# Three contraction steps of the down stage's first product placed beside the last channel tile, in place of one

## The chip, the cores and the metric

The kernel runs on one core of a Trainium2 chip. The metric is the device time of one execution in microseconds (us): the median of the runs of a kernel. Beside the timed runs there is one profiled execution, whose trace gives the rows quoted below; the times in them count from the start of its span.

## The reference

One encoder layer over two request groups (256 and 1024 tokens, model width 1024). The part that matters here is its last piece, a gated feed-forward block with a width-3 convolution along the tokens between its two products:

```
def conv_ffn(h, w_up, w_conv, b_conv, w_down):
    up = h @ w_up                                  # (tokens, 2 * 2816)
    up = lax.conv_general_dilated(up, w_conv...)   # depthwise, width 3, + b_conv
    gate, val = jnp.split(up, 2, axis=-1)
    return (jax.nn.silu(gate) * val) @ w_down      # (tokens, 1024)
...
h = rmsnorm(x, g_pre_ffn[l]) * (1 + scale2) + shift2
y = conv_ffn(h, w_up[l], w_conv[l], b_conv[l], w_down[l])
x = x + gate2 * rmsnorm(y, g_post_ffn[l])
```

All data are float32.

## The kernel before

Each float32 matmul operand is split into a high and a low part (`split`, lines 89 to 91: ScalarE, ACT, rounds the high part; VectorE, DVE, or GpSimd, POOL, subtracts it from the source for the low part), and TensorE (PE) makes three products of the parts. So one operand costs one instruction on ACT and then one on DVE or POOL.

**The up stage** goes over 22 channel tiles f of 128 channels, in the order 10 to 21 and then 0 to 9. For each tile four 256 KB pieces of `w_up` are loaded into four rotating slots (`raw`, 4 in all), sums of them are formed (`S`), and both are split into weight operands `ws`, which rotate through 8 slots (6 in the pool `wr`, 2 in `sf`). PE then makes seven products of 12 matmuls (line 1210), a Strassen-like scheme over two 512-token halves, in the order X(11), Y(12), X(S2), V(S1), X(S3), V(S4), X(22). X and V are accumulated on, and each intermediate state is read out by ACT or DVE (lines 1217 to 1233) before PE adds the next product to it: lines 1217 and 1223 copy X to `ug`, 1225 copies V to `uv`, 1227 adds X to `uv`, 1229 adds V to `ug`. While PE is at the next tile, ACT and DVE do convolution, SiLU and gating (`ag`, `av`, lines 1043 to 1245), and the result `av` is stored to `g_d[f]` in DRAM (line 1076). The last tile is f = 9; its store goes by POOL's queue.

**The down stage** makes seven more Strassen-like products (M3, M5, M1, M7, M4, M2, M6; line 1153), each of 11 contraction steps k and 5 token tiles j, 3 matmuls for each pair, so 15 matmuls for a step. Step k of the first product, M3, takes A00_k (loaded from `g_d[2k]`, 320 KB) and the difference of two 256 KB blocks of `w_down`, `raw_d01_k` and `B11_k`. Its operands are `aoM3_k` and `boM3_k`. The `A00` and `B11` tiles stay in memory for the later products. They lie in the pool `dr`, which is opened over the space of the pools `wr`, `wp`, `er` and others that the up stage has done with; the pool `dn` (the tiles `xo`, `G2`, `y`) is opened over `sf`.

**The early step.** For k = 0 of M3 the A tile is loaded as `ea_0` as soon as tile 0 is stored, and the two blocks of `w_down` as `raw_e` behind the loads of the last channel tile. `early_split` makes the operands `eao_0` and `ebo_0` in `er`, and PE runs the 15 matmuls right behind the last product of f = 9, while ACT and DVE still work on the convolution of f = 9. After that PE goes on with step 1.

**What sets the order.** PE runs in the order of the source. In this part the order on ACT, DVE, POOL and in the DMA queue of SyncE (SP) is chosen by a scheduler when the kernel is built. Each queue is worked through in order, so that an instruction that waits holds up all that stand behind it. Tiles that are opened over other tiles wait for the last use of these.

## Time and profile before

| | |
|---|---|
| median of 3 runs | 1454.65 us (1453.76 to 1455.06) |
| the profiled execution: its time, its span | 1453.5 us, 1451.8 us |
| PE busy | 1377.5 us, 95% of the span |
| DVE, ACT, POOL busy | 1031.5, 677.9, 546.8 us |
| granted TensorE clock, mean of the span | 0.980 |

In the rows, `start us, us` are the start and the length of a group of equal instructions; `[1.92 <-ACT uv L1225]` says that the engine stood idle for 1.92 us before them, until the named instruction ended. `PEld` is the loading of weights into PE, `SPq`, `ACTq` and `POOLq` are DMAs issued by those queues; the length in a DMA's row is that of its issue, not of its transfer. A row of stretches gives for each engine its busy time and in brackets the number of instructions, then the granted clock, the busy share of the DMA engines and what they moved.

### The profile page before, as it was taken

To read this page: it belongs to the slowest core of one execution; us is meant where nothing else is said; L and a number is where in the kernel's file an instruction comes from. 1 tells how busy PE (TensorE), PEld (TensorE's weight loads), DVE (VectorE), ACT (ScalarE), POOL (GpSimd) and SP (SyncE) were. 2 spreads that over 40 slices of the span, in tenths; PEclk is the share of its full clock that TensorE was granted. 3 is DMA by queue.
4 is the path that set the end of the run, shared out by engine and by line. 5 is a ranking of instruction groups with operands and counts; after the bars stand their busy time and mean duration, and the time that the engine had idled before them with its cause. 6 is when DMAs were issued, how large, how long until landed. Compare 5 with 4: busy or idle time off the path is not lost. (4 is left out here: it accounts for less than half of the span.)

```text
span 1451.8 us, 20330 instructions
## 1 busy us (share of the span) xinstructions
PE 1377.5 (95%) x7057; PEld 1132.6 (78%) x7057; DVE 1031.5 (71%) x1619; ACT 677.9 (47%) x1379; POOL 546.8 (38%) x664
## 2 busy tenths in 40 slices
PE   8999989898999999888999999999999989999996
PEld 6786667676788788877888888887888768888875
DVE  5675667878845456896657566678788576996777
ACT  3543465644433333565444454544555345533632
POOL 3346755787764111434333333344444100000301
PEclk9999999999999999999999999999999999999998
DMA  9657542332233632552221212122222478365764
GB/s 287 218 211 268 184 151 74 111 111 69 83 105 113 215 112 83 168 150 83 80 63 61 82 59 84 56 92 67 84 87 87 147 245 299 106 197 178 161 206 163
DMA packets 178011, 195.91 MB, mean 135 GB/s; under 512 B 12152, under 2 KB 132020, under 8 KB 175604
## 3 DMA queue, kind: packets, MB, share of 16 engines
q1 hardware_dynamic: 170760, 176.83, 37.9%
q10 hardware_dynamic: 5468, 14.38, 2.9%
q0 software_dynamic: 1680, 3.41, 1.3%
q8 instruction: 55, 0.90, 0.3%
q14 instruction: 48, 0.39, 0.1%
HBM read 156.55 MB, written 38.03 MB: 134 GB/s over the span
## 5 line engine op out<-in xcount | busy, mean ns | idle before, releaser
L1153 PE MATMUL dn<-boM,aoM 128*128 128x512 f32 x1140 | 268.2, 398 | 8.9 <-ACT boM L90 5.1
L1153 PEld LDWEIGHTS dn<-boM,aoM 128*128 128x128 f32 x1140 | 218.5, 192 | 58.6 <-ACT boM L90 6.4
L91 POOL TENSOR_TENSOR ws<-raw_s,ws 128x512 fp32r<-128x512 f32 x56 | 88.5, 1584 | 166.0 <-ACT ws L90 165.0
L91 POOL TENSOR_TENSOR ws_S<-S,ws_S 128x512 fp32r<-128x512 f32 x66 | 102.0, 1547 | 128.2 <-ACT ws_S L90 128.1
L1210 PE MATMUL upX<-bop_T,ws_S 128*128 128x512 f32 x528 | 130.5, 397 | 6.2 <-ACT ws_S L90 3.3
L1210 PEld LDWEIGHTS upX<-bop_T,ws_S 128*128 128x128 f32 x528 | 100.0, 191 | 27.7 <-ACT ws_S L90 3.5
L338 PE MATMUL ps_ga<-w_a,h1hi 128*128 128x512 f32 x320 | 104.6, 404 | 5.4 <-POOL w_a L91 4.4
L338 PE MATMUL ps_gb<-w_b,h1hi 128*128 128x512 f32 x320 | 105.0, 409 | 1.6 <-DVE w_b L91 1.1
L90 ACT ACTIVATE ws_S<-S 128x512 fp32r<-128x512 f32 x88 | 54.8, 629 | 76.7 <-PE upX L1210 27.6
L1043 DVE SCALAR_TENSOR_TENSOR ag<-ug,c,ag 128x1023 f32<-128x1023 f32 x44 | 67.7, 1540 | 24.1 <-ACT ag L1047 23.3
L338 PEld LDWEIGHTS ps_ga<-w_a,h1hi 128*128 128x128 f32 x320 | 59.3, 191 | 25.1 <-issue 6.7
L1201 PEld LDWEIGHTS upQ<-hp,ws 128*128 128x128 f32 x576 | 72.3, 191 | 1.9
L90 ACT ACTIVATE ws<-raw_s 128x512 fp32r<-128x512 f32 x78 | 48.6, 626 | 52.6 <-issue 26.2
L1201 PE MATMUL upQ<-hp,ws 128*128 128x256 f32 x576 | 72.8, 283 | 0.0
L1097 PE MATMUL upP<-hp,wp 128*128 128x256 f32 x480 | 62.1, 290 | 11.2 <-DVE wp L91 8.3
L1097 PEld LDWEIGHTS upP<-hp,wp 128*128 128x128 f32 x480 | 59.7, 196 | 13.3 <-DVE wp L91 9.5
L1178 DVE TENSOR_TENSOR S<-raw_s,raw_s 128x512 f32<-128x512 f32 x44 | 53.7, 1221 | 22.1 <-DMA raw_s<-in_w_up_dram 18.2
L90 ACT ACTIVATE aoM<-saM 128x640 fp32r<-128x640 f32 x55 | 40.4, 738 | 62.1 <-issue 24.5
L338 PEld LDWEIGHTS ps_gb<-w_b,h1hi 128*128 128x128 f32 x320 | 57.8, 191 | 14.6 <-issue 2.6
L97 POOL TENSOR_TENSOR rstd<-ms,mhalf 128x2 f32<-128x2 f32 (+1 forms) x90 | 65.7, 730 | 7.3
L880 PE MATMUL y<-wo,mh 128*128 128x512 f32 x160 | 64.0, 400 | 2.1 <-ACT mh L794 2.1
L1210 PE MATMUL upV<-bop,ws_S 128*128 128x512 f32 x264 | 63.6, 390 | 1.9 <-ACT uv L1225 1.9
(289 smaller groups left out, 3227.8 us busy)
## 6 DMA issues: line engine op xcount, KB each, us to landing
raw_d<-in_w_down_dram SPq DMA_DIRECT2D x103, 256.0 KB
raw_s<-in_w_up_dram SPq DMA_DIRECT2D x88, 256.0 KB
A<-g_d SPq DMA_DIRECT2D x66, 320.0 KB
wa<-in_w_ada_dram SPq DMA_DIRECT2D x16, 1024.0 KB
g_d<-av SPq DMA_DIRECT2D x21, 512.0 KB
raw_p<-in_w_up_dram SPq DMA_DIRECT2D x40, 256.0 KB
wa<-in_w_ada_dram SPq DMA_DIRECT2D x16, 512.0 KB
vr_d<-vr SPq DMA_DIRECT2D x20, 256.0 KB
```

The lines of the kernel that those rows point to most:

```text
L90: nc.scalar.activation(w[:, 0, :], raw, AF.Copy)
L91: (eng or nc.gpsimd).tensor_tensor(out=w[:, 1, :], in0=raw, in1=w[:, 0, :].bitcast(F32), op=ALU.subtract)
L97: nc.gpsimd.tensor_tensor(out=r, in0=ms, in1=mhalf.to_broadcast([P, n]) if n > 1 else mhalf, op=ALU.pow)
L338: nc.tensor.matmul(ps, st, mv, start=(i == 0), stop=(i == n - 1))
L880: nc.tensor.matmul(ys[n], mh[:, kt, :], wos[(kt, n)][:, 0, :], start=(i == 0), stop=False)
L1043: nc.vector.scalar_tensor_tensor(out=acc[:, o:o + b - a], in0=src[:, a:b], scalar=c2[:, i, fi:fi + 1], in1=acc[:, o:o + b - a], op0=ALU.mu ...
L1097: nc.tensor.matmul(ps[:, half, :], st, hp[:, hi, kt, :], start=(kt == 0 and i == 0 and half == 0), stop=(kt == KT - 1 and i == 2), skip_gr ...
L1153: nc.tensor.matmul(ps, ao[ai][:, cs_], w[wi], start=(k == 0 and q == 0), stop=(k == NK - 1 and q == 2))
L1178: nc.vector.tensor_tensor(out=s, in0=a, in1=b, op=op)
L1201: nc.tensor.matmul(Q[:, half, :], st, hp[:, hi, kt, :], start=(kt == 0 and i == 0 and half == 0), stop=(kt == KT - 1 and i == 2), skip_gro ...
L1210: nc.tensor.matmul(ps, w[:, wi, P * j:P * j + P], bops[(b, j)][:, hi, :], start=(start and j == 0 and i == 0), stop=(stop and j == 3 and i ...
```

## The change

`NE`, the number of early steps, goes from 1 to 3. The two operand parts of the A tile lie in `er` for k = 0 and 1 and in two slots of the pool `wp` for k = 2 (weight slots that the up stage no longer uses). The operand of the weights, `ebo_k`, takes the next of the 8 rotating `ws` slots in place of a place of its own in `er`. `ea` stays a single buffer, so the three A tiles follow each other through it.

```
-    NE = 1
+    NE = 3
...
     def early_split():
         for k, (a, b) in enumerate(eops):
             nc.vector.tensor_tensor(out=b[0], in0=b[0], in1=b[1], op=ALU.subtract)
-            ao = er.tile([P, 2, 640], F32R, name=f"eao_{k}")
-            bo_ = er.tile([P, 2, 512], F32R, name=f"ebo_{k}")
-            split(ao, a, nc.vector)
+            if k < 2:
+                t = er.tile([P, 2, 640], F32R, name=f"eao_{k}")
+                ao = [t[:, h, :] for h in range(2)]
+            else:
+                ao = [wp.tile([P, 2, 512], F32R, tag="w", name=f"eao{'hl'[h]}_{k}", bufs=5)
+                      .rearrange("p a c -> p (a c)")[:, 0:640] for h in range(2)]
+            bo_ = ws_slot(f"ebo_{k}")
+            nc.scalar.activation(ao[0], a, AF.Copy)
+            nc.vector.tensor_tensor(out=ao[1], in0=a, in1=ao[0].bitcast(F32), op=ALU.subtract)
             split(bo_, b[0], nc.vector)
-            eops[k] = [[t[:, h, :] for h in range(2)] for t in (ao, bo_)]
+            eops[k] = [ao, [bo_[:, h, :] for h in range(2)]]
+
+    def ws_slot(name):
+        i = wstate["i"] % 8
+        wstate["i"] += 1
+        return fslot(name) if i < 6 else sf.tile([P, 2, 512], F32R, tag="w", name=name, bufs=2)
...
         def wop(name, src, eng=None):
-            if wstate["i"] % 8 < 6:
-                w = fslot(f"ws{f}_{name}")
-            else:
-                w = sf.tile([P, 2, 512], F32R, tag="w", name=f"ws{f}_{name}", bufs=2)
-            wstate["i"] += 1
+            w = ws_slot(f"ws{f}_{name}")
             split(w, src, eng)
             wops[name] = w
```

Seven lines are added ahead of the later code, so line 1217 before is 1224 in the change, and so on. The scheduler moves instructions at three places. The number in a name after the step or tile counts tiles and can be passed over; `[waits ...]` names the counters that the instruction waits for: an engine's, or one of the eight of the hardware DMA queues (`DMAHW`) and of the software ones (`DMASW`).

The first place is ACT in the up stage, where it works for tiles 3 and 4. Before:

```order
L90 ACTIVATE ws4_S4_10067<-S4_4_10065 128x512 [waits DVE_49,PE_49]
L90 ACTIVATE ws4_22_10070<-raw_s4_11_10041 128x512 [waits DMAHW4_49,PE_49,Pool_49]
L1047 ACTIVATE ag3_10025<-ug3_9932,c2_5061 128x1024 [waits DVE_49,Activation_49]
L1233 ACTIVATE uv3_9933<-upX_3_9929 128x512 [waits PE_49]
L90 ACTIVATE ws5_11_10188<-raw_s5_00_10179 128x512 [waits DMAHW5_49]
L1047 ACTIVATE av3_10026<-uv3_9933,c2_5061 128x1024 [waits DMAHW2_49,Activation_49]
L1243 ACTIVATE ag3_10025<-ag3_10025 128x1024 [waits DVE_49]
```

In the change:

```order
L90 ACTIVATE ws4_S4_10067<-S4_4_10065 128x512 [waits DVE_49,PE_49]
L1144 ACTIVATE eao_1_10918<-ea_1_10772 128x640 [waits DMAHW1_49]
L90 ACTIVATE ws4_22_10070<-raw_s4_11_10041 128x512 [waits DMAHW4_49,PE_49,Pool_49]
L1047 ACTIVATE ag3_10025<-ug3_9932,c2_5061 128x1024 [waits DVE_49,Activation_49]
L1240 ACTIVATE uv3_9933<-upX_3_9929 128x512 [waits PE_49]
L90 ACTIVATE ws5_11_10188<-raw_s5_00_10179 128x512 [waits DMAHW5_49]
L1047 ACTIVATE av3_10026<-uv3_9933,c2_5061 128x1024 [waits DMAHW2_49,Activation_49]
L1250 ACTIVATE ag3_10025<-ag3_10025 128x1024 [waits DVE_49]
L1224 ACTIVATE ug4_10076<-upX_4_10073 128x512 [waits PE_49]
```

The high part of `eao_1` now stands between `ws4_S4` and `ws4_22`; its low part stands on DVE at the same place, ahead of the addition that ends `ug3`. The load of `ea_1` is issued by SP two loads behind the store of tile 2, for whose landing it waits. `eao_0` stands in both kernels two tiles earlier, between `ws2_S4` and `ws2_22`.

The second place is DVE beside tiles 8 and 9, where `raw_e` is subtracted. Before:

```order
L1178 TENSOR_TENSOR S4_9_10794<-raw_s9_01_10757,S2_9_10781 128x512 [waits DMAHW2_49,Pool_49]
L1136 TENSOR_TENSOR raw_e0_0_10768<-raw_e0_0_10768,raw_e0_1_10769 128x512 [waits DMAHW6_49,DMAHW7_49,DVE_49,Pool_49]
L91 TENSOR_TENSOR ebo_0_10900<-raw_e0_0_10768,ebo_0_10900 128x512 [waits Activation_49]
L91 TENSOR_TENSOR ws9_S3_10791<-S3_9_10789,ws9_S3_10791 128x512 [waits PE_49,Activation_49]
L1227 TENSOR_TENSOR uv8_10653<-upX_8_10649,uv8_10653 128x512 [waits PE_49]
```

In the change:

```order
L1185 TENSOR_TENSOR S4_9_10806<-raw_s9_01_10757,S2_9_10793 128x512 [waits DMAHW4_49,Pool_49]
L1136 TENSOR_TENSOR raw_e0_0_10768<-raw_e0_0_10768,raw_e0_1_10769 128x512 [waits DMAHW0_49,DMAHW1_49,DVE_49,Pool_49]
L91 TENSOR_TENSOR ws9_S3_10803<-S3_9_10801,ws9_S3_10803 128x512 [waits PE_49,Activation_49]
L1136 TENSOR_TENSOR raw_e1_0_10774<-raw_e1_0_10774,raw_e1_1_10775 128x512 [waits DMAHW3_49,DMAHW4_49,DVE_49,Pool_49]
L1234 TENSOR_TENSOR uv8_10653<-upX_8_10649,uv8_10653 128x512 [waits PE_49]
```

The split of `ebo_0` is gone from here (it stands some rows lower, and on ACT behind the copies of V and X of tile 8, no longer ahead of that of V), and the subtraction of `raw_e1` has come in ahead of the addition that reads X of tile 8. One half of `raw_e1` takes the slot of `raw_e0_1`, so its load waits for the subtraction two rows higher.

The third place is the SP queue at the change of stages. Before:

```order
L1076 DMA g_d8_72<-av8_10746 128x2x512 [waits DVE_49]
L1293 DMA A00_1_10983<-g_d2_66 128x640 [waits DMAHW6_49,PE_49]
L1308 DMA B11_1_10984<-in_w_down_dram 128x512
L1293 DMA A00_2_10981<-g_d4_68 128x640 [waits DMAHW0_49]
L1308 DMA B11_2_10982<-in_w_down_dram 128x512 [waits DMAHW1_49]
```

In the change:

```order
L1076 DMA g_d8_72<-av8_10746 128x2x512 [waits DMAHW2_49,DVE_49]
L1315 DMA raw_d01_6_11134<-in_w_down_dram 128x512 [waits DMAHW3_49,DVE_49]
L1372 DMA xo1_13289<-out_0_dram 128x1024 [waits DMAHW2_49,DMAHW5_49,DMASW2_49,DVE_49]
L1300 DMA A00_3_11040<-g_d6_70 128x640 [waits PE_49]
L1315 DMA B11_3_11041<-in_w_down_dram 128x512 [waits DMAHW7_49]
L1300 DMA A00_4_11038<-g_d8_72 128x640 [waits DMAHW0_49,PE_49]
```

A 512 KB load for the end of the kernel, `xo1`, has come in ahead of the first A tile of M3. Its place in memory is that of `av9`, the last channel tile's result, and `DMASW2_49` counts the landing of the store of `g_d9` from it. `A00_1` waited for PE's first reading of `ws9_12`, early in tile 9. `A00_3` lies over the slot of `eaoh_2`, and what it waits for on PE is the last but one of the 45 early matmuls; `A00_4` waits for the last.

## The prediction

> **What bounds the kernel now.** I read the page's busy times and costliest groups first:

> ```profile
> PE 1377.5 (95%) x7057; PEld 1132.6 (78%) x7057; DVE 1031.5 (71%) x1619; ACT 677.9 (47%) x1379; POOL 546.8 (38%) x664
> L1153 PE MATMUL dn<-boM,aoM 128*128 128x512 f32 x1140 | 268.2, 398 | 8.9 <-ACT boM L90 5.1
> ```

> TensorE (PE) is the bound, so only its idle time and its slow clock can be won or lost. In the down products 5.1 of 8.9 us idle end with ACT's `boM`. The timeline of PE shows where:

> ```profile
> 1157.74 2.88 PE L1210 MATMUL upX<-bop_T,ws 128*128 128x512 f32 x12
> 1160.46 3.56 PE L1153 MATMUL dn<-ebo,eao 128*128 128x512 f32 x15
> 1168.56 46.77 PE L1153 MATMUL dn<-boM,aoM 128*128 128x512 f32 x191 [4.54 <-ACT boM L90]
> ```

> Call 1160.46 t0. A row's length runs to the modelled end of its last matmul; starts are the safe measure: 12 matmuls take 1160.46 - 1157.74 = 2.72, so 0.2267 each at full rate. After the early step PE waits 4.54 us for step 1. The view by stretches shows what follows (PE first; the granted clock is the third figure from the end):

> ```profile
> 1168.56:1175.00 6.44, 6.44 (x14) 4.76 (x15) 5.27 (x9) 2.40 (x4) 0.00 (x0) 0.50 0.94 318
> ```

> PE restarts at clock 0.50: 14 matmuls in 6.44 us where 3.17 would do, so 3.27 lost. The hand-over thus holds 4.54 + 3.27 = 7.8 us to be won. It is the place the change goes for; two more waits in the up stage must be read, since instructions for the early steps lie in those queues.

> **Hand-over to M3.** Before, 45 matmuls (k = 0 to 2) were through at 1175.00 + 16 x 0.2267 = 1178.63, t0 + 18.2. In the change k = 0 to 2 run without a pause, to t0 + 45 x 0.2267 = t0 + 10.2 plus the last one's tail, 10.4. Step 3 must then be ready. But `A00_3` lies over `eaoh_2`, and SP issues it only at the last but one early matmul, about t0 + 10.5; ahead of it in SP stands `xo1`, waiting for the store of `g_d9`:

> ```profile
> 1165.28 1.23 DVE L1245 TENSOR_TENSOR av<-ag,av 128x1024 f32<-128x1024 f32 x1
> 1166.81 0.81 POOL L1076 DMA_DIRECT2D g_d<-av  x1 [28.60 <-DVE av L1245]
> g_d<-av POOLq DMA_DIRECT2D x1, 512.0 KB, 3.6
> ```

> The store lands at 1166.81 + 3.6 = 1170.4 = t0 + 10.0: nearly the same time, so both waits would have to go. Behind the issue come the load and the operands. How long a 320 KB load takes is seen at `ea` of tile 0 (SP, then its readers on ACT and DVE; the store ahead of it too):

> ```profile
> 993.75 0.37 SPq L1076 DMA_DIRECT2D g_d<-av  x1
> 997.80 0.34 SPq L1128 DMA_DIRECT2D ea<-g_d  x1
> 1000.90 0.74 ACT L90 ACTIVATE eao<-ea 128x640 fp32r<-128x640 f32 x1 [3.48 <-DMA ea<-g_d]
> 1001.68 0.82 DVE L91 TENSOR_TENSOR eao<-ea,eao 128x640 fp32r<-128x640 f32 x1 [4.19 <-ACT eao L90]
> ```

> Load: 1000.90 - 997.80 = 3.1. Store of 512 KB to the load that waits for it: 4.05. From the A tile to PE, the rows of step 1:

> ```profile
> 1166.43 0.82 DVE L91 TENSOR_TENSOR aoM<-A,aoM 128x640 fp32r<-128x640 f32 x1
> 1167.16 0.68 DVE L1330 TENSOR_TENSOR sbM<-raw_d,B 128x512 f32<-128x512 f32 x1
> 1167.88 0.63 ACT L90 ACTIVATE boM<-sbM 128x512 fp32r<-128x512 f32 x1 [2.93 <-DVE sbM L1330]
> ```

> 0.74 on ACT, then 1168.56 - 1166.43 = 2.13: 2.9 in all. Lower bound of the start of k = 3: t0 + 10.5 + 3.1 + 2.9 = 16.5. With `xo1`'s 512 KB moved first, 4.05 - 3.1 = 0.95 more: 17.5. Upper: G2, 1 MB, which ACT now issues early, since `aoM` of steps 1 and 2 no longer stands ahead of it, shares the DMA engines: 19.3. Its own passage before is seen in ACT's queue, in SP and among the waits:

> ```profile
> 1167.89 0.36 ACTq L1267 DMA_DIRECT2D G<-gate_d  x1
> SPq L1293 <- DMA G<-gate_d: 5.8, 1, 5.8
> 1176.68 0.33 SPq L1293 DMA_DIRECT2D A<-g_d  x1
> ```

> So G2 takes 1176.68 - 1167.89 = 8.8 us beside other loads. I take t0 + 17.6, a pause of 7.2 in place of 4.54. Work done, that is 0.6 ahead of before; but the slow restart, which before lay inside these 45 matmuls, now comes behind them. It cost 3.27 there; at tile 2, below, 3.42 us at half clock lost 1.7. Middle 2.5. **Term: -0.6 + 2.5 = +1.9**, from 16.5 - 18.2 + 1.7 = 0 to 19.3 - 18.2 + 3.3 = +4.4.

> **Tile 4: the split of `eao_1`.** Before has the same thing once, for `eao_0`:

> ```profile
> 1004.75 2.88 PE L1210 MATMUL upY<-bop,ws 128*128 128x512 f32 x12
> 1009.62 4.22 PE L1210 MATMUL upX<-bop_T,ws_S 128*128 128x512 f32 x12 [1.99 <-ACT ug L1217]
> 1013.64 2.65 PE L1210 MATMUL upV<-bop_T,ws_S 128*128 128x512 f32 x9
> 1011.15:1014.57 3.42, 3.42 (x10) 2.68 (x9) 3.42 (x3) 0.69 (x2) 2.62 (x2) 0.50 0.00 0
> 1004.48 3.52 DVE L1043 SCALAR_TENSOR_TENSOR ag<-ug,c,ag 128x1023 f32<-128x1023 f32 x2 [0.78 <-ACT ag L1047]
> ```

> ACT waited 3.48 and DVE 4.19 for `ea_0`; everything behind (the taps of `ag`, SiLU, the copy `ug`) came late, and PE stood 1.99 before X(S2). Half clock followed. X(S2) should have started at 1007.47, V at 1010.19; V came at 1013.64: 3.45 lost, 2.15 stall and 1.3 clock. The change adds this for tile 2. There before was:

> ```profile
> 1035.76 0.37 SPq L1076 DMA_DIRECT2D g_d<-av  x1
> 1041.48 0.69 DVE L1229 TENSOR_TENSOR ug<-upV,ug 128x512 f32<-128x512 f32 x1 [2.03 <-PE upV L1210]
> 1043.82 2.60 DVE L1043 SCALAR_TENSOR_TENSOR ag<-ug,c,ag 128x1023 f32<-128x1023 f32 x2 [0.93 <-ACT ag L1047]
> 1046.46 1.06 ACT L1243 ACTIVATE ag<-ag 128x1024 f32<-128x1024 f32 x1
> 1047.43 0.58 ACT L1217 ACTIVATE ug<-upX 128x512 f32<-128x512 f32 x1
> 1049.44 2.88 PE L1210 MATMUL upX<-bop_T,ws_S 128*128 128x512 f32 x12
> ```

> `ea_1` is issued at 1035.76 + 4.05 = 1039.81 and lands at 1042.9; ACT 0.78 and DVE 0.8 on, the addition into `ug` starts at 1044.5 in place of 1041.48: 3.0 late. The copy `ug` ended at 1048.01, 1.4 before PE's need. So PE waits 3.0 - 1.4 = 1.6, and 2.5 if the taps take 3.52 as at tile 2; 1.3 if the load lands a little sooner. I take 1.9, nearer to the first row. The 1.3 of clock may come or not: 0.6. **Term: +2.5**, 1.3 to 3.8. Queued behind the waiting split are also the splits of `ws4_22` and `ws5_11`; PE needs these later than `ug`.

> **Tile 8: the subtraction of `raw_e1`.**

> ```profile
> 1134.68 0.63 ACT L90 ACTIVATE ebo<-raw_e 128x512 fp32r<-128x512 f32 x1 [5.04 <-DVE raw_e L1136]
> 1135.85 3.02 PE L1210 MATMUL upV<-bop,ws_S 128*128 128x512 f32 x12 [1.92 <-ACT uv L1225]
> 1138.70 2.88 PE L1210 MATMUL upX<-bop_T,ws 128*128 128x512 f32 x12
> 1129.88 0.82 SPq L1131 DMA_DIRECT2D raw_e<-in_w_down_dram  x2
> 1133.95 0.69 DVE L1136 TENSOR_TENSOR raw_e<-raw_e,raw_e 128x512 f32<-128x512 f32 x1 [1.32 <-DMA raw_e<-in_w_down_dram]
> 1134.67 0.33 SPq L1308 DMA_DIRECT2D raw_d<-in_w_down_dram  x1
> ```

> Removed: ACT no longer waits for `raw_e` ahead of the copy of V, so the 1.92 goes. Added: DVE takes the addition into `uv` of tile 8, on which X(S3), the row at 1138.70, depends, only after `raw_e1`, whose second half is loaded when the first subtraction is over (1134.64; SP issued `raw_d` then). It lands 3.1 later by `ea`, or 3.65 by `raw_e`'s second load (1130.3 to 1133.95): 1137.8 to 1138.3. Subtraction and addition, 0.69 each: X(S3) starts at 1139.2 to 1139.7, 0.5 to 1.0 later than before. The stall isn't gone but moved, in one piece of some 2.8. I take +0.7, and 0.5 for the clock, which 1.99 idle halved and 1.92 didn't. **Term: +1.2**, 0 (a landing as quick as the old wait allowed) to 2.7.

> **The rest, at nothing.** Eight split instructions more, 0.6 to 0.8 each, stand in tiles 2 to 9 or replace those of M3's steps 1 and 2; in tile 9 DVE has room:

> ```profile
> 1155.29 0.69 DVE L1227 TENSOR_TENSOR uv<-upX,uv 128x512 f32<-128x512 f32 x1 [7.22 <-PE upX L1210]
> ```

> Without that cover two ebo splits would cost 2 x 0.68. `A00_1`, `A00_2` and their `B11` are loaded a second time for M5: 1.15 MB, at the 318 GB/s that end the half-clock row above 3.6 us of DMA under 37 us (165 x 0.2267) of matmuls; uncovered, one landing, 3.1. The ws slots taken by `ebo` delay the next weight operand by one place of eight; a tile's seven products give it 7 x 2.72 = 19 us.

> **Sum.** 1.9 + 2.5 + 1.2 = +5.6 against the profiled execution's 1453.5: 1459.1. Its time is 1.15 below the median of the runs; on that it would be 1460.25. I forecast between, **1459.7**.

> **Rivals.** *The other side, faster.* If `A00_3` is issued before t0 + 4.4 (10.4 - 2.9 - 3.1), step 3 is ready as the early steps end: 7.8 is won, and with +2.5 and +1.2 the time is 1453.5 - 4.1 = 1449.4. For it: the 4.54 is really waiting for operands. Against: the row of `A00_3` names a PE count inside the early steps, and `xo1` needs a store landing at t0 + 10. Chance 6%. *Nothing to be seen.* The lower ends at tile 8 and the hand-over (0 and 0) with 1.3 to 2.5 of tile 4: 1454.8 to 1457. For it: the pause buys 30 matmuls. 15%. *The clock is kinder.* Tile 8's 1.92 left the clock at 1.00, so a short wait may leave it there, and the restart may cost tile 2's 1.7: 1.9 + 0.7 - 0.6 + 1.7 = +3.7, 1457.2 to 1458.4. Against: tile 2's 1.99 did halve it. 17%. *G2 in the way.* If its 8.8 us hold store, `xo1` and `A00_3` as they held an A load for 5.8, half of that stands before k = 3: t0 + 20.5 and a full restart, -18.2 + 20.5 + 3.3 + 3.7 = +9.3: 1462.8 to 1464. 12%. My forecast has 50%.

> [...]

> **How the numbers follow.** 0.2%, about what a measurement can tell, is 2.9: below 1451.7 is faster, above 1457.6 slower. Slower: 50 + 12 + most of 17, 77%; no change: 15 and the rest, 17%; faster 6%. Range: 1455.2 (leaving out the faster case and the quietest part) to 1464.0 (the upper bounds together).

> **What would show it.** A wait of 1.3 to 2.5 before X(S2) of tile 4, ended by ACT's `ug`; before X(S3) of tile 8 one ended by DVE's `uv`, and none before its V; a group of 45 early matmuls, then some 7 us idle and a clock of 0.50; SP's `xo` load near t0 + 10 with `A` behind it. The prediction is wrong if `A` is issued well before t0 + 10, or if ACT's `eao` of tile 4 doesn't wait.

## The result, and the profile after

The change takes 1459.22 us in the median of 10 runs (1456.14 to 1466.79), the kernel before 1452.78 in the median of 10 (1449.17 to 1455.06). The ratio is 1.0051, with a 95% interval of 1.0036 to 1.0066: slower by 7.4 us, 5.2 to 9.6. The forecast was 1459.7 and slower. The profiled execution of the change took 1460.14 us, that of before 1453.5.

The busy times and the costliest group of the change, from its page:

```profile
PE 1371.9 (94%) x7057; PEld 1129.9 (77%) x7057; DVE 1033.2 (71%) x1619; ACT 678.6 (47%) x1379; POOL 544.4 (37%) x664
L1164 PE MATMUL dn<-boM,aoM 128*128 128x512 f32 x1110 | 257.5, 393 | 14.2 <-ACT boM L90 9.4
```

PE has no more work than before, but its idle time ahead of the down products went from 8.9 to 14.2 us, of which 9.4 now end with `boM`. Where it stands is seen in the timeline of PE (start, length, what, in brackets the idle time before it):

```profile
1046.85 2.88 PE L1217 MATMUL upY<-bop,ws 128*128 128x512 f32 x12
1051.50 3.06 PE L1217 MATMUL upX<-bop_T,ws_S 128*128 128x512 f32 x12 [1.76 <-ACT ug L1224]
...
1135.99 2.88 PE L1217 MATMUL upV<-bop,ws_S 128*128 128x512 f32 x12
1141.72 4.20 PE L1217 MATMUL upX<-bop_T,ws 128*128 128x512 f32 x12 [2.85 <-DVE uv L1234]
...
1165.26 6.96 PE L1164 MATMUL dn<-ebo,eao 128*128 128x512 f32 x30
...
1184.12 16.05 PE L1164 MATMUL dn<-boM,aoM 128*128 128x512 f32 x61 [8.50 <-ACT boM L90]
```

The row of 30 early matmuls holds steps 0 and 1; the 15 of step 2 read `eaoh` and `eaol`, have rows of their own and follow without a pause. The three waits stand where the prediction put them: 1.76 at tile 4, ended by ACT's `ug`, and 2.85 at tile 8, ended by DVE's `uv`, both as it named them, and 8.50 behind the 45 early matmuls. The 1.92 before V(S4) of tile 8 is gone. (The prediction calls the group that waits at tile 8, the row at 1138.70 of before, X(S3). It is the next product on X, X(22); the addition that it waits for reads X(S3).)

The first matmul of a stretch is a safe mark, so the two profiles can be laid beside each other between such marks (us, worked out from the starts in the two timelines of PE). A loss "by spacing" is, here and below, the distance between the starts of two products less the 2.72 that 12 matmuls take:

| from, to | before | change | difference |
|---|---|---|---|
| start to Y of tile 2 | 1004.75 | 1006.26 | +1.51 |
| Y of tile 2 to Y of tile 4 | 41.97 | 40.59 | -1.38 |
| Y of tile 4 to V(S4) of tile 8, before's wait for `uv` (2.08 by spacing) left out | 87.05 | 89.14 | +2.09 |
| from there to Y of tile 9, with that wait | 10.37 | 12.95 | +2.58 |
| Y of tile 9 to the first early matmul | 16.32 | 16.32 | 0 |
| early matmuls to step 5 of M3 | 25.01 | 27.72 | +2.71 |
| step 5 of M3 to the first matmul of M2 | 170.00 | 170.00 | 0 |
| M2 | 43.97 | 42.28 | -1.69 |
| M6 and the end of the span | 52.36 | 53.14 | +0.78 |

The sum is +6.6, the difference of the two spans. Three rows, +2.09, +2.58 and +2.71, are the change's; they make 7.4, what the ratio gives. The rows of tile 2 and M2, -1.38 and -1.69, lie at waits that the change doesn't touch: both kernels have them, and less slow clock followed here (0.50 for 3.41 us at tile 2 of before, none in the change; 0.50 for 6.83 us in M2 of before, for 3.41 in that of the change). The first and the last row vary from kernel to kernel: over the twelve profiles of this document the first stretch takes from 1001.8 to 1008.0 and the last from 51.5 to 54.5, and +1.51 and +0.78 can't be told from that. That these four rows add up to no more than -0.8 is chance.

### The profile page after: what moved, and what is told of

It is laid out like the page before. It is cut to its first block, busy times and chain, and to the rows that moved or that the text cites. A ratio compares the mean times of both kernels' runs of the same rounds, so it can differ in the third digit from the quotient of the medians.

```text
span 1458.4 us, 20331 instructions
## 1 busy us (share of the span) xinstructions
PE 1371.9 (94%) x7057; PEld 1129.9 (77%) x7057; DVE 1033.2 (71%) x1619; ACT 678.6 (47%) x1379; POOL 544.4 (37%) x664
## 3 DMA queue, kind: packets, MB, share of 16 engines
q0 software_dynamic: 1680, 3.41, 1.3%
## 4 chain that ended last, share of the span: by engine, by line
PE 59%; DVE 15%; POOL 7%; issue 7%; DMA 7%; ACT 5%; POOLq 0%; SPq 0%; ACTq 0%; DVEq 0%
PE upX L1217 14%; PE dn L1164 12%; PE upV L1217 7%; PE upQ L1208 5%; PE ps_gb L338 3%; PE upY L1217 3%; PE ps_ga L338 3%; PE y L880 2%; PE y L881 2%; PE y L883 2%; DVE St L724 2%; DMA raw_d<-in_w_down_dram 1%; POOL rstd L97 1%; PE ps_qkS L347 1%; POOL w_a L91 1%
## 5 line engine op out<-in xcount | busy, mean ns | idle before, releaser
L1164 PE MATMUL dn<-boM,aoM 128*128 128x512 f32 x1110 | 257.5, 393 | 14.2 <-ACT boM L90 9.4
L1164 PEld LDWEIGHTS dn<-boM,aoM 128*128 128x128 f32 x1110 | 210.0, 190 | 61.6 <-ACT boM L90 10.7
L91 POOL TENSOR_TENSOR ws<-raw_s,ws 128x512 fp32r<-128x512 f32 x56 | 86.0, 1539 | 171.8 <-ACT ws L90 170.3
L91 POOL TENSOR_TENSOR ws_S<-S,ws_S 128x512 fp32r<-128x512 f32 x66 | 103.3, 1567 | 123.5 <-ACT ws_S L90 123.2
L1217 PE MATMUL upX<-bop_T,ws_S 128*128 128x512 f32 x528 | 130.1, 396 | 8.0 <-ACT ug L1224 4.0
L1217 PEld LDWEIGHTS upX<-bop_T,ws_S 128*128 128x128 f32 x528 | 99.5, 191 | 29.9 <-ACT ug L1224 4.8
L90 ACT ACTIVATE ws_S<-S 128x512 fp32r<-128x512 f32 x88 | 54.9, 629 | 75.1 <-PE upX L1217 29.1
L1043 DVE SCALAR_TENSOR_TENSOR ag<-ug,c,ag 128x1023 f32<-128x1023 f32 x44 | 68.4, 1553 | 24.1 <-ACT ag L1047 23.3
L90 ACT ACTIVATE ws<-raw_s 128x512 fp32r<-128x512 f32 x78 | 48.5, 625 | 51.3 <-issue 27.1
L90 ACT ACTIVATE aoM<-saM 128x640 fp32r<-128x640 f32 x55 | 40.4, 739 | 63.0 <-issue 24.5
L1185 DVE TENSOR_TENSOR S<-raw_s,raw_s 128x512 f32<-128x512 f32 x44 | 53.3, 1211 | 21.4 <-DMA raw_s<-in_w_up_dram 17.5
L1217 PE MATMUL upX<-bop_T,ws 128*128 128x512 f32 x264 | 65.1, 396 | 2.8 <-DVE uv L1234 2.8
## 6 DMA issues: line engine op xcount, KB each, us to landing
g_d<-av SPq DMA_DIRECT2D x21, 512.0 KB
wa<-in_w_ada_dram SPq DMA_DIRECT2D x16, 512.0 KB
```

The lines of the kernel that those rows point to most:

```text
L90: nc.scalar.activation(w[:, 0, :], raw, AF.Copy)
L91: (eng or nc.gpsimd).tensor_tensor(out=w[:, 1, :], in0=raw, in1=w[:, 0, :].bitcast(F32), op=ALU.subtract)
L1043: nc.vector.scalar_tensor_tensor(out=acc[:, o:o + b - a], in0=src[:, a:b], scalar=c2[:, i, fi:fi + 1], in1=acc[:, o:o + b - a], op0=ALU.mu ...
L1164: nc.tensor.matmul(ps, ao[ai][:, cs_], w[wi], start=(k == 0 and q == 0), stop=(k == NK - 1 and q == 2))
L1185: nc.vector.tensor_tensor(out=s, in0=a, in1=b, op=op)
L1217: nc.tensor.matmul(ps, w[:, wi, P * j:P * j + P], bops[(b, j)][:, hi, :], start=(start and j == 0 and i == 0), stop=(stop and j == 3 and i ...
```

## The experiments

Medians are compared with 1459.22 for the change, which was not timed again beside the experiments. Each group of experiments has its own runs of the kernel before (medians of 1450.8 to 1451.6, for 1452.78 beside the change), so the ratio to before is given too.

**1. The two holds at the hand-over.** The first edit lays the tiles of steps 3 to 5 over space that isn't held:

```
-    for k in range(NK - 1, NE - 1, -1):
-        new_ar(0, k)
-        if k < 7:
-            new_br(k)
+    new_ar(0, 10), new_br(6)
+    for k in (3, 4):
+        new_ar(0, k), new_br(k)
+    for k in (5, 9, 8, 7, 6):
+        new_ar(0, k)
+    new_br(5)
```

The second puts the load of `xo1` behind M3's last A tile in the SP queue (`am` keeps the A loads):

```
-        nc.sync.dma_start(xo, out_rows(t))
+        with tc.issue_after(am[(0, NK - 1)].ins):
+            nc.sync.dma_start(xo, out_rows(t))
```

The first alone:

> The change, with one edit: the A00 and B11 tiles of M3's steps 3 to 5 are laid over space that is free before the early matmuls (the order of the tiles in the pool is permuted), so that A00_3 to A00_5 wait for no early matmul; xo1 stays ahead of them in the SP queue. In the profile of the change xo1 was issued at 1175.02, 9.8 us after the first early matmul, and A00_3 0.4 us later. Two holds, each enough (as predicted): nothing changes, the pause of PE before step 3 stays at 7.5 to 9 us, the time within 2 us of the change's 1459.2. Rival, the held space alone is the hold: the pause goes, 1459.2 - 8.7 - 2.2 = 1448.3. Rival, the loads' bandwidth alone: pause of 7 to 8.

1458.93 us, ratio 1.0049 (1.0031 to 1.0068): 0.3 less, nothing that can be told from the change. From its SP queue, and its PE:

```profile
1172.89 0.33 SPq L1374 DMA_DIRECT2D xo<-out_dram  x1
1173.27 0.42 SPq L1302 DMA_DIRECT2D A<-g_d  x1
```

```profile
1163.24 6.96 PE L1164 MATMUL dn<-ebo,eao 128*128 128x512 f32 x30
1180.99 34.25 PE L1164 MATMUL dn<-boM,aoM 128*128 128x512 f32 x141 [7.39 <-ACT boM L90]
```

`A` is still issued 10.0 us after the first early matmul, directly behind `xo`. The pause, 7.39, is 1.1 shorter than in the profile of the change and just below what was expected.

The second alone:

> The change, with one edit: the load of xo1 is issued behind the last A tile of M3 instead of ahead of the first; the space of A00_3 and A00_4 is still held by the early matmuls. Two holds: A00_3 is issued at the last but one early matmul, 10.1 to 10.5 us after the first as before, and only xo1's 512 KB (about 1.0 us, from the store and load of tile 0) no longer go ahead of it: pause of 6.5 to 8 us, time 1456.5 to 1459. Rival, xo1's wait for the store is the hold: the pause shrinks below 3 us, time near 1450.

1457.32 us, ratio 1.0040 (1.0028 to 1.0053). SP, then PE:

```profile
1171.91 0.33 SPq L1301 DMA_DIRECT2D A<-g_d  x1
```

```profile
1161.74 6.96 PE L1164 MATMUL dn<-ebo,eao 128*128 128x512 f32 x30
1178.19 36.98 PE L1164 MATMUL dn<-boM,aoM 128*128 128x512 f32 x152 [6.09 <-ACT boM L90]
```

`A` waits until 10.2 us after the first early matmul, now for the matmuls that read `eaoh_2`. The pause is 6.1, a little below what was expected: from the issue of `A` to PE it takes 6.28 us, in the change 8.70.

Both together:

> The change, with both edits: free space for steps 3 to 5 and xo1 behind M3's A tiles. Two holds: A00_3 is issued before the first early matmul (as soon as X(S3) of tile 9 has read its weights), step 3 is ready before the 45 early matmuls end, the pause and the slow restart go together: 8.66 us of spacing and about 2.2 of half clock (61 matmuls took 16.05 - in place of 13.8 - us), so 1459.2 - 10.9 = 1448.3, range 1446 to 1451. Rival, G2's 1 MB or the DMA supply set the start: a pause of 4 us or more stays, time above 1452.

1446.95 us, ratio 0.9972 (0.9956 to 0.9987), 12.3 below the change and now faster than before. SP and PE:

```profile
1158.30 0.33 SPq L1303 DMA_DIRECT2D A<-g_d  x1
```

```profile
1163.55 6.96 PE L1164 MATMUL dn<-ebo,eao 128*128 128x512 f32 x30
1173.75 41.42 PE L1164 MATMUL dn<-boM,aoM 128*128 128x512 f32 x182
```

The A tile is issued 5.25 us ahead of the first early matmul, step 3 follows the 45 matmuls after 10.20 us = 45 x 0.2267 without a pause, and the slow restart is gone with it (182 matmuls in 41.42 us). So there were two holds in a row, each enough by itself: the edits alone gave 0.3 and 1.9, both together 12.3 (11.5 by the ratios).

**2. Two early steps.** The edit is `NE = 2` in place of 3.

> The change with two early steps in place of three; the pool wp is then not used, and the build puts no xo1 ahead of the A tiles. 30 early matmuls end 6.8 us after the first; step 2's operands come from DVE behind the gating of tile 9 (ended 6.1 us after the first early matmul in the change's profile): first matmul of step 2 at 7.5 to 9 us, a pause of 0.7 to 2.2 and no half clock or little. The stalls at tiles 4 and 8 stay. 1459.2 - 8.7 - 2.2 + 1.5 = 1449.8, range 1447.5 to 1452.5. Rival, the pause belongs to the early steps whatever holds them: about as the change, 1457 to 1461.

1449.99 us, ratio 0.9990 (0.9976 to 1.0004). Step 2 came 7.36 us after the first early matmul, a little sooner than expected, and the pauses were 0.40 and 0.77:

```profile
1170.16 6.96 PE L1164 MATMUL dn<-ebo,eao 128*128 128x512 f32 x30
1177.52 0.50 PE L1164 MATMUL dn<-boM,aoM 128*128 128x512 f32 x1 [0.40 <-ACT boM L90]
1178.80 36.58 PE L1164 MATMUL dn<-boM,aoM 128*128 128x512 f32 x160 [0.77 <-DVE boM L91]
```

So a further early step as such doesn't bring the pause. This build lacks both the third step's operands and the early `xo1`; experiment 1 shows that each of them is enough. The waits at tiles 4 and 8 stay in this kernel (2.05 and 2.96 by spacing) and eat what the hand-over wins.

**3. Tile 4 alone.** The splits of `eao_1` are ordered behind the copy of X(S2) and the addition of X(S3) of tile 4 (`mk` keeps these two of each tile, and what stands under `behind(f)` is ordered behind both, on ACT and on DVE):

```
-            nc.scalar.activation(ao[0], a, AF.Copy)
-            nc.vector.tensor_tensor(out=ao[1], in0=a, in1=..., op=ALU.subtract)
+            with behind({1: 4}.get(k)):
+                nc.scalar.activation(ao[0], a, AF.Copy)
+                nc.vector.tensor_tensor(out=ao[1], in0=a, in1=..., op=ALU.subtract)
```

> The change, with one edit: the two split instructions of eao_1 are ordered behind the copy of X(S2) on ACT and behind the addition of X(S3) on DVE, both of tile 4, when ea_1 has long landed. Predicted term: without it the wait before X(S2) of tile 4 (1.76 us in the change's profile, 1.93 by spacing; 1.86 to 2.05 by spacing in the four kernels run since) goes, and what half clock follows it in some executions. 1.9 to 2.5 less than the change: 1459.2 - 2.2 = 1457.0. Rival, PE waits for something else there (the weights ws4_22 or the taps in any case): the wait stays above 1 us and the time within 1 us of the change.

1456.63 us, ratio 1.0036 (1.0023 to 1.0049): 2.6 less than the change, 2.2 by the ratios. In its timeline X(S2) of tile 4 follows Y after 2.72 us, without a wait:

```profile
1044.09 2.88 PE L1225 MATMUL upY<-bop,ws 128*128 128x512 f32 x12
1046.81 2.88 PE L1225 MATMUL upX<-bop_T,ws_S 128*128 128x512 f32 x12
```

The intervals of the two kernels overlap, so the time alone would not prove 2; the profile shows that the wait left and that none took its place.

**4. Tile 8 alone.** The subtraction of `raw_e1` (and `raw_e2`) is ordered behind the addition of X(S3) into `uv` of tile 8:

```
-            nc.vector.tensor_tensor(out=b[0], in0=b[0], in1=b[1], op=ALU.subtract)
+            with behind(8 if k else None):
+                nc.vector.tensor_tensor(out=b[0], in0=b[0], in1=b[1], op=ALU.subtract)
```

> The change, with one edit: the subtraction of raw_e1 (and of raw_e2) is ordered on DVE behind the addition of X(S3) into uv of tile 8. Predicted term +1.2 against the kernel before, which itself loses 2.08 there. The change loses at tile 8 3.01 us by spacing and 1.3 at clock 0.69 (12 matmuls in 4.00 in place of 2.72 us). Theory, the place in DVE's queue is the cause: no wait before X(22) of tile 8, 3 to 4.3 less than the change, 1459.2 - 3.7 = 1455.5. Rival, raw_e1's late landing comes back later (ebo_1 late for the early matmuls or raw_d late): an idle of 1 us or more before or among the 45 early matmuls, and less than 1.5 won.

1456.48 us, ratio 1.0037 (1.0026 to 1.0048): 2.7 less than the change, 2.0 by the ratios, not 3.7. The wait itself is gone:

```profile
1134.35 2.88 PE L1225 MATMUL upV<-bop,ws_S 128*128 128x512 f32 x12
1137.07 2.88 PE L1225 MATMUL upX<-bop_T,ws 128*128 128x512 f32 x12
```

The early matmuls ran without an idle, so the rival's late `ebo_1` didn't come. The expectation took the 1.3 of slow clock of one profile for a fixed price; in four other profiles this wait came with it (2.75 and 2.80 us idle, then 4.44 and 4.45 for the 12 matmuls) and without it (2.42 and 3.55 us idle, then 2.90 and 2.89). The wait alone is 3.0 by spacing, more than the medians show; the two intervals are wide enough for that, and experiment 6 gives 5.5 for tiles 4 and 8 together.

**5. One early step, `ebo_0` in a ws slot.** `NE = 1` in the changed code: what is left of the change is the place of `ebo_0` and of its split.

> The changed code with one early step, as before; what is left of the change is that ebo_0 lies in a ws slot, and that by this its split stands on ACT behind the copies of V and X of tile 8. The kernel before waits there for raw_e: 2.08 us by spacing before V(S4) of tile 8. Theory: that wait goes and nothing comes for it: 2.1 less than before, 1451.3 - 2.1 = 1449.2 (range 1448 to 1450.5). Rival, the late split delays the early matmuls: an idle before these and the same time as before, 1451.3.

1448.73 us, ratio 0.9988 (0.9977 to 0.9999): 2.1 below its runs of before, 1450.84. The wait before V(S4) of tile 8 is not in its profile. So the part of the change that the prediction counted as removed is worth about its 2.1 (1.7 by the ratio, 0.1 to 3.3 by its interval); in the full change the subtraction of `raw_e1` takes its place and more.

**6. The three repairs together**, and then a fourth, the same ordering for `eao_0` behind tile 2's copies (`{0: 2, 1: 4}`), which mends a wait that the kernel before has too.

> The change with all repairs so far: free space for steps 3 to 5, xo1 behind the A tiles, eao_1's split behind tile 4's copies, raw_e1's subtraction behind tile 8's addition. If the terms add, it is the previous combination's 1446.95 less 2.0 (tile 4) and less 3.0 to 4.0 (tile 8): 1441.5, range 1439 to 1443.5, about 10 us or 0.7% below the kernel before. Of the four places only tile 2's wait (2.0 to 2.4 by spacing) is left. Rival, the gains overlap, since a wait taken out of the up stage comes back at the next wait (steps 3 to 5 then are not ready when the early matmuls end): 1444 to 1447.

1441.41 us, ratio 0.9935 (0.9921 to 0.9949). The gains add: 5.5 on top of the hand-over's 12.3.

> The three-step kernel with all repairs, and eao_0's split ordered behind the copies of tile 2 as eao_1's behind those of tile 4. What the kernel before already lost at tile 2 (2.15 us by spacing and 1.3 of half clock; 1.91 to 2.38 by spacing in the kernels run since) should go: 1441.4 - 2.2 to 3.5 = 1437.9 to 1439.2, take 1438.7. Rival, that wait was covered by the next one: 1441.

1440.66 us, ratio 0.9922 (0.9909 to 0.9935), 0.75 less, 1.9 by the ratios. In its profile tile 2 has no wait, and from Y of tile 2 to Y of tile 4 it takes 38.08 in place of 40.13. That is 2.05, the wait alone, and no slow clock was there to be won in the kernel that it is compared with (1.00 from 1009.70 to 1015.00). Less than expected, and within the noise of the two medians.

This is the best kernel of the study, 10.9 us or 0.8% faster than before. The same repairs with one early step:

> One early step as before, with ebo_0 in a ws slot and eao_0's split behind the copies of tile 2: all repairs of the up stage, without the two further early steps. 1448.7 - 2.7 = 1446.0 (1445 to 1447.5); the pause of 4.5 us before step 1 and its slow restart stay. The difference to the kernel with three free early steps is what these two steps are worth by themselves: 4.70 by spacing and some 2.5 of half clock, 7.2. Rival, the slow restart is not part of it: 4.7.

1446.64 us, ratio 0.9969 (0.9958 to 0.9981). Its pause is that of before:

```profile
1151.38 3.56 PE L1172 MATMUL dn<-ebo,eao 128*128 128x512 f32 x15
1159.48 5.91 PE L1172 MATMUL dn<-boM,aoM 128*128 128x512 f32 x13 [4.54 <-ACT boM L90]
```

So the two further early steps, with nothing that holds the next ones, are worth 1446.64 - 1440.66 = 6.0 us (6.8 by the ratios), between the 4.7 of the pause alone and the 7.2 with its slow restart.

## Why the prediction was right, and where its sizes were off

The forecast of 1459.7 was +5.6 on the profile, moved up halfway to the median of three runs; measured were 1459.22 and, by the ratio, +7.4. The time agrees better than the difference: the runs of before came out 1.9 lower with ten runs than with three. That the time was met within 0.5 us is luck, since the terms were 1.8 too small and the time of before that they were added to, 1454.1, was 1.3 too high. The mechanism of each term is what the profiles show; two sizes were off.

**Tile 4, predicted +2.5, measured +2.09 (profile) and 2.2 to 2.6 (by undoing it).** Every step of the chain is there. SP, ACT and DVE of the change:

```profile
1035.89 0.37 SPq L1076 DMA_DIRECT2D g_d<-av  x1
1039.91 0.34 SPq L1128 DMA_DIRECT2D ea<-g_d  x1
```

```profile
1042.78 0.74 ACT L1144 ACTIVATE eao<-ea 128x640 fp32r<-128x640 f32 x1 [3.25 <-DMA ea<-g_d]
1050.87 0.58 ACT L1224 ACTIVATE ug<-upX 128x512 f32<-128x512 f32 x1
```

```profile
1043.55 0.83 DVE L1145 TENSOR_TENSOR eao<-ea,eao 128x640 fp32r<-128x640 f32 x1 [3.97 <-ACT eao L1144]
1044.29 0.68 DVE L1236 TENSOR_TENSOR ug<-upV,ug 128x512 f32<-128x512 f32 x1
```

Issue 4.02 behind the store (taken: 4.05), landing 2.87 later (3.1), the addition at 1044.29 (1044.5), PE 1.76 idle or 1.93 by spacing (1.9). The 0.6 for the clock didn't come here (1.00 from 1051.00 to 1058.10).

**Tile 8, predicted +1.2, measured +2.58.** The wait was sized right, the slow clock behind it too small. DVE:

```profile
1136.11 0.69 DVE L1136 TENSOR_TENSOR raw_e<-raw_e,raw_e 128x512 f32<-128x512 f32 x1 [1.24 <-DMA raw_e<-in_w_down_dram]
1140.37 0.69 DVE L1136 TENSOR_TENSOR raw_e<-raw_e,raw_e 128x512 f32<-128x512 f32 x1 [2.97 <-DMA raw_e<-in_w_down_dram]
1140.98 0.68 DVE L1234 TENSOR_TENSOR uv<-upX,uv 128x512 f32<-128x512 f32 x1
```

The first subtraction ends at 1136.80, and the second could begin at 1140.37, 3.6 later (bounds 3.1 and 3.65, the upper end). X(22) started at 1141.72. On before's time (V(S4) 2.22 earlier) that is 1139.50, 0.80 behind before's 1138.70: 0.7 was taken. The rest, 1.8, is slow clock, for which 0.5 stood: behind the one long stall the clock was halved in this profile (0.50 from 1143.26 to 1146.67), as the term's upper end allowed. What went with this is in the last section.

**The hand-over, predicted +1.9, measured +2.71.** The issue of `A` was right: `xo` at 9.8 and `A` at 10.2 us after the first early matmul, for 10.0 and 10.5. Step 3 started at 18.9 in place of 17.6; that is the step that was mis-sized. SP, DVE and ACT of the change:

```profile
1175.02 0.33 SPq L1372 DMA_DIRECT2D xo<-out_dram  x1
1175.42 0.40 SPq L1300 DMA_DIRECT2D A<-g_d  x1
1175.86 0.43 SPq L1315 DMA_DIRECT2D B<-in_w_down_dram  x1
```

```profile
1180.18 0.82 DVE L91 TENSOR_TENSOR aoM<-A,aoM 128x640 fp32r<-128x640 f32 x1 [8.88 <-ACT aoM L90]
1181.99 0.69 DVE L1337 TENSOR_TENSOR sbM<-raw_d,B 128x512 f32<-128x512 f32 x1 [0.98 <-DMA B<-in_w_down_dram]
```

```profile
1179.42 0.74 ACT L90 ACTIVATE aoM<-A 128x640 fp32r<-128x640 f32 x1 [10.92 <-DMA A<-g_d]
1182.81 0.74 ACT L90 ACTIVATE aoM<-A 128x640 fp32r<-128x640 f32 x1 [2.66 <-DMA A<-g_d]
1183.45 0.61 ACT L90 ACTIVATE boM<-sbM 128x512 fp32r<-128x512 f32 x1
```

The A tile landed 4.0 after its issue, as taken with `xo1` ahead of it. But the prediction let everything behind that go as in before, 2.9 from the A tile to PE. Here it took 4.7. For `boM` DVE waited for `B` until 1181.99, 6.1 after its issue. And in ACT's queue the `aoM` of the next step stands ahead of `boM`, so that the A tile of that step counts too: it landed 7.4 after the issue of the first. With `xo1` out of the queue it landed after 5.0, and the way from issue to PE was 6.28, 2.4 shorter, where 0.95 was priced; with `xo1` there but other space, after 6.4, and the way was 7.72, 1.4 longer than without `xo1`. So one 512 KB load ahead of a group of loads delayed the last of the operands by more than the 0.95 taken for its own passage; why by 1.4 in one kernel and 2.4 in the other is open. Behind step 3 the restart (clock 0.50 from 1180.80 to 1187.63) cost 2.06 to step 5, for which 2.5 had been taken.

**The rivals.** *Faster* was kept away by both holds; the two edits show that it is what comes when they are gone. *Nothing to be seen* asked for 0 at the hand-over and at tile 8, where 2.71 and 2.58 came. *The kinder clock* held at tile 4 (1.00) but not at tile 8 (0.50). *G2 in the way* did not come. By stretches (fourth to last: clock; last: GB/s):

```profile
1168.00:1170.00 2.00, 2.00 (x10) 1.67 (x9) 1.94 (x2) 0.50 (x1) 0.00 (x0) 1.00 0.82 246
1170.00:1172.00 2.00, 2.00 (x10) 1.67 (x9) 1.23 (x1) 0.00 (x0) 0.40 (x1) 1.00 0.69 274
1174.00:1176.00 2.00, 1.62 (x8) 1.00 (x6) 0.00 (x0) 0.00 (x0) 0.00 (x0) 1.00 0.20 72
1176.00:1178.00 2.00, 0.00 (x0) 0.00 (x0) 0.00 (x0) 0.00 (x0) 0.00 (x0) 1.00 0.95 323
```

246 and 274 GB/s for 2 us each are 1.04 MB: G2, issued at 1167.44, had all but its last few KB moved by 1172, 4.6 later, and when `A` was issued at 1175.42 the DMA engines stood nearly free (0.20). The 8.8 of before were a passage among other loads (DMA engines 0.94 busy from 1168.56 to 1175.00). The reloads for M5 and the further splits cost nothing: from step 5 of M3 to M2 both kernels take 170.00.

## What to carry to other kernels

When work is moved ahead, look at what its operands lie over and who is queued behind what: the next step's first load waited for space that the moved work itself still read, and a load for the kernel's end with a late wait had come in ahead of it. Two such holds in a row hid each other here, so that mending one showed next to nothing (0.3 and 1.9 of 12.3 us); take both away before giving the idea up. A split that the scheduler placed early, ahead of its load's landing, held up what stood behind it in its queue (at tile 4 ACT waited 3.25 us for `ea` and DVE 3.97 for ACT, and PE then 1.76 for `ug`), and an order edge behind the next urgent copy freed it here without a new wait.

## What the runs showed of the hardware

In these profiles the length of a wait alone doesn't tell whether the clock is halved after it. The wait at tile 8 in the kernel with `xo1` late, then in the one with the space alone:

```profile
1139.81 3.06 PE L1217 MATMUL upX<-bop_T,ws 128*128 128x512 f32 x12 [3.55 <-DVE uv L1234]
```

```profile
1139.72 4.61 PE L1217 MATMUL upX<-bop_T,ws 128*128 128x512 f32 x12 [2.75 <-DVE uv L1234]
```

3.55 us idle kept the full clock (1.00 from 1139.81 to 1142.70), 2.75 lost it (0.62 in the mean from 1139.72 to 1144.16); before's 1.99 at tile 2 lost it (0.50 from 1011.15 to 1014.57), and the change's 2.21 at the same place kept it (1.00 from 1011.36 to 1014.40):

```profile
1011.36 3.01 PE L1217 MATMUL upX<-bop_T,ws_S 128*128 128x512 f32 x12 [2.21 <-ACT ug L1224]
1014.21 2.88 PE L1217 MATMUL upV<-bop_T,ws_S 128*128 128x512 f32 x12
```

12 matmuls there took 2.85 us, at before 1013.64 - 1009.62 = 4.02.

```profile
1134.62:1138.03 3.41, 1.64 (x8) 1.02 (x6) 1.54 (x1) 0.63 (x1) 0.99 (x1) 1.00 0.33 98
1138.03:1141.44 3.41, 1.63 (x7) 1.35 (x8) 2.49 (x4) 0.99 (x1) 0.00 (x0) 1.00 0.25 77
1141.44:1144.86 3.42, 3.42 (x17) 2.81 (x16) 3.10 (x3) 2.21 (x4) 0.00 (x0) 1.00 0.27 77
```

```profile
1136.93:1140.34 3.41, 0.66 (x4) 0.53 (x4) 2.00 (x5) 0.63 (x1) 0.00 (x0) 1.00 0.18 56
1140.34:1143.76 3.42, 3.42 (x10) 2.65 (x9) 2.61 (x3) 1.24 (x1) 0.00 (x0) 0.50 0.44 143
```

The 3.55 is split between two stretches, in each of which PE was busy for 1.63 us or more, and the next ran at 1.00. The 2.75 left PE busy for 0.66 of one stretch, and the next ran at 0.50. Before's wait of 1.92 at tile 8 left 1.60, and the next ran at 1.00:

```profile
1134.03:1137.45 3.42, 1.60 (x7) 1.34 (x8) 2.42 (x4) 2.15 (x4) 0.54 (x1) 1.00 0.66 196
1137.45:1140.86 3.41, 3.41 (x17) 2.83 (x16) 1.57 (x3) 1.81 (x2) 0.75 (x1) 1.00 0.18 61
```

Of the other waits in the profiles of before and of the change, before's 1.99 at tile 2 left 1.52 of a stretch (1007.74 to 1011.15) and the change's 2.85 at tile 8 1.54 (1139.84 to 1143.26), and the next ran at 0.50; the change's 2.21 at tile 2 left 2.19 (1010.14 to 1013.55) and its 1.76 at tile 4 2.05 (1047.68 to 1051.10), and the next ran at 1.00. So of these seven waits the ones that left 1.54 us or less of a stretch lost the clock for the next, and the ones that left 1.60 or more kept it. That holds for these waits and shows no bound: in M6 of before a stretch with PE busy for 2.04 us (1424.16 to 1427.58) was followed by one at 0.50, and no run places the waits on purpose.

A slow stretch cost 1.74 us at tile 2 of before (1016.80 - 1009.62 for two products, less 2 x 2.72) and 1.78 at tile 8 of the change (1148.94 - 1141.72, less the same): that is the 1.8 there. The restart of before went through two of them, the first with PE busy for 3.02 us (1168.17 to 1171.58), the second for all of its 3.41; that of the change went through one (1184.22 to 1187.63, busy for 3.26), and the next ran at 1.00.

Since the grid stood elsewhere in the two traces, the same wait may cost some 1.8 us more in one execution than in the next, by the author's estimate from the 1.74 and 1.78. The spread of the runs fits with it, which is argued and not shown: the ten runs of the change span 10.7 us, with a mean clock of 0.972 in the two slowest and 0.982 in one of the two fastest; 26 runs of the kernel before span 8.4.
